# Gates of a bidirectional recurrence made where the projections end, with its diagonal, two copies and a scaling moved to other places

## The chip, the cores and the metric

The kernel runs on one core of a Trainium2 chip. A core has a matrix engine (TensorE, "PE" in the profile), a vector engine (VectorE, "DVE"), a scalar engine (ScalarE, "ACT"), GpSimd ("POOL"), and a synchronisation engine (SyncE, "SP") that here only issues transfers. Transfers are also issued from GpSimd, where they can add to what lies at the destination. Each engine works through its own queue in order; semaphores tie the queues together. The metric is the device time of one execution in microseconds, with the median over several runs.

## What is computed

One layer of an encoder trunk on 1024 positions of 1024 values in float32. After an RMS norm, one projection makes the columns of all token mixers. A convolution branch (GLU, 31 taps, LayerNorm, swish, pointwise product) and a bidirectional gated linear recurrence (HGRN2, 8 heads of 128) run on them, are gated, merged and projected; a gated feed-forward block with a 3-tap convolution follows. The parts that the change touches:

```python
def _forget_log_and_key(z, lb):
    zf = z.astype(jnp.float32)
    f = lb + (1.0 - lb) * jax.nn.sigmoid(zf)
    lf = jnp.log(jnp.clip(f, MIN_FORGET, 1.0))
    key_gate = (1.0 - lb) * jax.nn.sigmoid(-zf)
    return lf, key_gate

def _token_mixers(...):
    proj = jnp.einsum("bsd,de->bse", h, w_in)
    glu_in, q, v, z_f, z_b, og, g_a, g_b = jnp.split(proj, SPLIT_POINTS, axis=-1)
    a = jax.nn.glu(glu_in, axis=-1)
    a = _dwconv_centred(a, dw_w, dw_b)
    a = jax.nn.silu(_layernorm(a, ln_w, ln_b))
    a = jnp.einsum("bsc,cd->bsd", a, pw_w)
    o = _bi_hgrn2(q, v, z_f, z_b, lb[0], lb[1])
    of = o * lax.rsqrt(jnp.mean(o * o, axis=-1, keepdims=True) + EPS)
    of = of.reshape(o.shape[0], o.shape[1], HGRN_WIDTH) * norm_w.astype(jnp.float32)
    bmix = (of * jax.nn.silu(og.astype(jnp.float32))).astype(h.dtype)
    ...
```

For each head and direction the recurrence is `S_t = diag(f_t) S_{t-1} + k_t v_t^T`, `o_t = S_t^T q_t`. The kernel evaluates it for halves of 512 positions: inside blocks of 8 positions by two products, and across blocks by levels of 8, 16, 32 and 64.

## The kernel before

A product of float32 matrices is made of three passes: each operand is split into a high part (a cast on ACT, L121) and the remainder (a subtraction, mostly on DVE, L118), and L143 to L145 multiply high by high, high by low, low by high.

The stages follow one another with overlaps.

- *Projections in pairs* (up to about 480 us). `pair_job` (L224 to L285) makes two columns of 128 outputs for both halves with seven products instead of eight. Sums of weight blocks are made by accumulating transfers issued from GpSimd (L238). Products are gathered in three PSUM banks; `copy` (L266) takes partial sums p1, u2 and p7 out with ACT, and `evac` hands each quadrant (column, half) to the column's own function, in the order (0,0), (1,1), (1,0), (0,1). Of the seventeen pairs, 0 to 7 make q and the output gates, 8 to 16 make v, zf and zb of heads 0 to 5 (the list `todo`). `store` (L584) is the function of all these columns: DVE combines two partial sums (L588) into one of the three `ev` pages, or ACT copies a bank (L593), and SP writes the page to memory.
- *Convolution branch* beside it: the 31 taps on DVE (L645), then, for each half, the LayerNorm (L662 to L701): a mean (L672), a subtraction on DVE (L674), four squares on ACT into the four `tm` pages (L678), their sum on POOL (L657, L659), column sums on PE (L420), the rstd on POOL (L404, L405), its spread to all partitions (L411 to L413), and scale, shift and swish (L685 to L687). `s_pairs.fill(n)` puts n steps of the pair jobs between these.
- *Scan* (about 545 to 1000 us): 8 heads of two halves. `scan_inputs` loads q and z, makes k and f on ACT, and clamps f on DVE; `scan_base` makes cumulative products inside the blocks of 8, in the tile `DE`; `scan_levels` makes the 128 x 128 score blocks S, one level at a time, with masks; `scan_states` and `outputs` make the states that are carried; `scan_outputs` makes the head's outputs, their norm and gate. `between` (L1022) interleaves, after each step, dense projection steps (heads 6 and 7, merge gates), two steps of the next half's base, and one of the previous head's outputs.
- *Output projections, feed-forward up* (to about 1610 us), not touched.
- *Down projection*: five groups (4, 4, 5, 5, 4 blocks of 128 rows); `load_g` (L1234) loads and splits the next group's activations while the present one is multiplied.

The order of PE's instructions is written out by hand: it is the order in which the program calls them. The order on the other engines is a scheduler's. Pages of a pool are reused when their readers are done: `tm` has four, `ev` three.

Of the kernel before, what the change touches and what calls it, by code (L numbers as in the profile page):

```python
# [44 lines left out]
def tile_hybrid_encoder(  # L45
# [60 lines left out]
    def ev():  # L106
        return page(mp, "ev", 3)
# [280 lines left out]
    d_z = scratch("d_z", 2, NH, 2)  # L388
# [168 lines left out]
    m_32 = cp.tile([P, P], U8, name="m_32")  # L557

    def build_masks():
# [16 lines left out]
        for m, h in ((m_16, 16.0), (m_32, 32.0)):  # L576
            V.tensor_scalar(fs[:, 2, :], fs[:, 0, :], h, None, op0=ALU.is_ge)
            V.tensor_scalar(fs[:, 3, :], fs[:, 0, :], 2 * h, None, op0=ALU.is_lt)
            V.tensor_tensor(m, fs[:, 2, :], fs[:, 3, :], op=ALU.mult)
# [4 lines left out]
    def store(dst, func=None):  # L584
# [12 lines left out]

    todo = [
# [10 lines left out]
        for t in (  # L609
            (OFF_V + h * DK, store(d_v[h])),  # L610
            (OFF_ZF + h * DK, store(d_z[0][h])),
            (OFF_ZB + h * DK, store(d_z[1][h])),
# [128 lines left out]
    def scan_inputs(i):  # L741


# [3 lines left out]
        kk = hp.tile([P, 2, H], F32, tag="k", name=nm("k"), bufs=2)  # L747
        nc.sync.dma_start(q, d_q[h][half])
        for d in range(2):
            z = page(hp, "zi", 3)  # L750
            nc.sync.dma_start(z, d_z[d][h][half])
            A.activation(kk[:, d, :], z, AF.Sigmoid, scale=-1.0)
            A.activation(z, z, AF.Sigmoid)
            fo = view(f, d * H + 7 * d, [[8, NB], [1 - 2 * d, 8]])
            A.activation(
                fo,
                z.rearrange("p (b e) -> p b e", e=8),
                AF.Identity,
                scale=oml_of(d, h),
                bias=lb_of(d, h),  # L760
            )
        V.tensor_scalar(f, f, MIN_FORGET, 1.0, op0=ALU.max, op1=ALU.min)
        return q, f, kk, kscale[:, h : h + NH + 1 : NH]

    def scan_base(ins):
# [14 lines left out]
        V.tensor_copy(ed(2, D + 4), fv(3, 4))  # L780
# [44 lines left out]
    def scan_levels(base, S_t, Tt):  # L825
# [31 lines left out]
        for h in (8, 16, 32, 64):  # L857
# [10 lines left out]
            elif h < 64:  # L868
                V.copy_predicated(S_t, over(m_16 if h == 16 else m_32), b)
# [15 lines left out]
        V.tensor_tensor(S_t, S_t, c4(dg), op=ALU.add)  # L885
# [40 lines left out]
    def scan_outputs(h, kept, Sf, Sb):  # L926


        ons, gates = [], [load(d_og[h][half]) for half in range(2)]
        for half in range(2):  # L930
# [22 lines left out]
            for c in range(4):  # L953
                sl = slice(c * P, (c + 1) * P)
                A.activation(on[:, sl], on[:, sl], AF.Copy, scale=rs[:, c : c + 1])
            ons.append(on)
            yield
        for half in range(2):
            if half:
                yield  # L960
# [365 lines left out]
    for n, group in enumerate(groups):  # L1326
        last = n == len(groups) - 1
        for hs in ((0,), (1,)) if last else ((0, 1),):
# [4 lines left out]
            if not last:  # L1333
                load_g(f0 + group, groups[n + 1])
# [36 lines left out]
```

## Time and profile before

| | us |
|---|---|
| median of three runs | 1889.1 (1888.84 to 1890.98) |
| the profiled execution's own time | 1889.98 |
| its span in the trace | 1888.2 |
| TensorE busy | 1790.4 |
| VectorE busy | 1270.7 |
| ScalarE busy | 797.8 |
| GpSimd busy | 212.4 |
| mean granted TensorE clock | 0.982 |

How to read it: the page gives for each engine its busy time, its share of the span and its instructions. A group line gives line, engine, operation, tiles and shape, then the busy time and the mean of one in ns, and behind the second bar the idle time of the engine ahead of these instructions with what ended it. A line of waits says which engine waited at which line for which other, in total, how often, and the longest. A line of the timeline has the start in the span, the duration, and in brackets the idle time before. "PEld" is the loading of weights, which overlaps the products. "d_z", "d_q" and the like are scratch arrays in memory.

### The profile page before, as it was taken

Reading aid. Unit: us, or ns where it says so; the run is one execution under the profiler, and the core shown is the slowest. Engines: PE = TensorE matmul, PEld = TensorE weight load, DVE = VectorE, ACT = ScalarE, POOL = GpSimd, SP = SyncE. Lnnn points to the kernel's source line nnn. Section 1 sums busy time; section 2 is a strip of 40 time slices with the busy share of each in tenths; the row PEclk is TensorE's granted clock in tenths of the full one; section 3 lists DMA queues with packets and bytes.
Section 4 is the critical chain, followed back from the end, with each engine's and each line's share of the span. In section 5 each row is a group of like instructions: output and inputs, shape, how many; then the busy total and the mean of one; then the engine's idle time right before and its main releaser. Section 6 shows DMA issues by size and latency. Waiting matters only on the chain. (4 is left out here: it accounts for less than half of the span.)

```text
span 1888.2 us, 23731 instructions
## 1 busy us (share of the span) xinstructions
PE 1790.4 (95%) x8543; PEld 1477.7 (78%) x8543; DVE 1270.7 (67%) x1860; ACT 797.8 (42%) x1488; POOL 212.4 (11%) x218
## 2 busy tenths in 40 slices
PE   6988999999999999999999999899999999899996
PEld 5767888877788887888877888678888888788885
DVE  3488999535469898999936555766676666534445
ACT  6333343234555555665443134544343434522124
POOL 3101111213100001000000000211111111000000
PEclk8999999999999999999999999999999999999998
DMA  7747788776562333332228665777676665733125
GB/s 261 221 118 169 182 195 195 180 180 159 185 200 85 117 97 106 112 110 81 82 69 251 193 197 174 178 159 154 145 156 147 146 148 129 218 96 95 55 85 167
DMA packets 322764, 282.99 MB, mean 150 GB/s; under 512 B 14798, under 2 KB 244950, under 8 KB 322646
## 3 DMA queue, kind: packets, MB, share of 16 engines
q1 hardware_dynamic: 270854, 240.57, 41.1%
q0 software_dynamic: 51792, 40.90, 15.3%
q8 instruction: 67, 1.10, 0.2%
q14 instruction: 51, 0.42, 0.1%
HBM read 189.14 MB, written 71.83 MB: 138 GB/s over the span
## 5 line engine op out<-in xcount | busy, mean ns | idle before, releaser
L143 PE MATMUL mm<-hx,wp 128*128 128x512 f32 x1176 | 481.1, 409 | 21.9 <-ACT xr L1244 4.8
L145 PE MATMUL mm<-hx,wp 128*128 128x512 f32 x1176 | 466.6, 397 | 4.6 <-DVE wp L118 4.6
L144 PE MATMUL mm<-hx,wp 128*128 128x512 f32 x1176 | 466.5, 397 | 2.1 <-POOL hx L118 1.9
L121 ACT CAST wp<-wr 128x1024 fp32r<-128x1024 f32 (+2 forms) x196 | 179.6, 917 | 337.9 <-PE mm L144 203.7
L118 DVE TENSOR_TENSOR wp<-wr,wp 128x1024 fp32r<-128x1024 f32 (+2 forms) x196 | 207.0, 1056 | 119.9 <-ACT wp L121 114.3
L143 PEld LDWEIGHTS mm<-hx,wp 128*128 128x128 f32 x1176 | 225.7, 192 | 72.2 <-ACT su L266 5.8
L145 PEld LDWEIGHTS mm<-hx,wp 128*128 128x128 f32 x1176 | 225.1, 191 | 55.7 <-DVE wp L118 6.7
L144 PEld LDWEIGHTS mm<-hx,wp 128*128 128x128 f32 x1176 | 225.7, 192 | 47.7 <-POOL hx L118 3.6
L645 DVE SCALAR_TENSOR_TENSOR acc<-gl,v_b,acc 128x1024 f32<-128x1024 f32 x120 | 149.1, 1277 | 0.5
L238 POOL DMA_DIRECT2D wr<-sw x39 | 34.9, 895 | 512.9 <-DVE wp L118 251.9
L1250 DVE TENSOR_TENSOR xr<-mm,xr 128x512 f32<-128x512 f32 x48 | 33.2, 691 | 82.0 <-PE mm L145 81.9
L838 PEld LDWEIGHTS sc<-qF,A 128*128 128x128 f32 x512 | 65.3, 192 | 19.1 <-issue 13.3
L838 PE MATMUL sc<-qF,A 128*128 128x128 f32 x512 | 68.2, 276 | 11.7 <-DVE qF L730 10.6
L121 ACT CAST wq<-sw 128x1024 fp32r<-128x1024 f32 x39 | 41.0, 1051 | 80.0 <-PE mm L144 62.8
L143 PE MATMUL mm<-hy,wp 128*128 128x512 f32 x156 | 62.2, 399 | 8.9 <-ACT wp L121 5.9
L835 ACT COPY A<-kG 128x512 f32<-128x512 f32 x64 | 39.7, 621 | 66.6 <-DVE kG L730 38.0
L1172 DVE SCALAR_TENSOR_TENSOR tm<-gp,v_a,tm 128x512 f32<-128x512 f32 x88 | 65.6, 746 | 1.7 <-ACT tm L1168 0.9
L266 ACT COPY su<-mm 128x512 f32<-128x512 f32 x78 | 45.4, 581 | 48.7 <-PE mm L145 48.5
L144 PE MATMUL mm<-hy,wp 128*128 128x512 f32 x156 | 61.8, 396 | 0.0
L145 PE MATMUL mm<-hy,wp 128*128 128x512 f32 x156 | 61.3, 393 | 0.0
L143 PE MATMUL tr<-hx,wp 128*128 128x512 f32 x156 | 61.2, 392 | 0.0
L143 PE MATMUL sc<-hy,wq 128*128 128x512 f32 x156 | 61.1, 392 | 0.0
(289 smaller groups left out, 3602.1 us busy)
## 6 DMA issues: line engine op xcount, KB each, us to landing
wr<-in_w_in_dram SPq DMA_DIRECT2D x55, 512.0 KB, 6.6
sw<-in_ffn_w_up_dram SPq DMA_DIRECT2D x44, 256.0 KB, 4.1
sw<-in_ffn_w_up_dram POOLq DMA_DIRECT2D x22, 512.0 KB, 8.5
wr<-in_ffn_w_up_dram SPq DMA_DIRECT2D x22, 512.0 KB, 4.9
d_g<-ft SPq DMA_DIRECT2D x44, 256.0 KB, 5.9
ev<-d_g SPq DMA_DIRECT2D x44, 256.0 KB, 3.1
wr<-sw POOLq DMA_DIRECT2D x39, 256.0 KB, 3.3
wr<-wr POOLq DMA_DIRECT2D x39, 256.0 KB, 4.4
```

Of the source, the lines that this page charges most:

```text
L118: eng.tensor_tensor(lo, src, hi.bitcast(F32), op=ALU.subtract)
L121: A.copy(hi, src)
L143: T.matmul(acc, whi[:, k, :], ahi, start=first, stop=False, skip_group_check=again)
L144: T.matmul(acc, whi[:, k, :], alo, start=False, stop=False, skip_group_check=again)
L145: T.matmul(acc, wlo[:, k, :], ahi, start=False, stop=last, skip_group_check=again)
L238: G.dma_start(o, a, accum_op=ALU.add)
L266: A.copy(t, acc)
L645: V.scalar_tensor_tensor(acc, g[:, k : k + S], tap(k), acc, op0=ALU.mult, op1=ALU.add)
L835: A.copy(A_t.rearrange("p (b x e) -> p b x e", x=2, e=h), pairs(kG, h))
L838: T.matmul(b[:, c * P : (c + 1) * P].rearrange("p (b x e) -> p b x e", x=2, e=h), A_t[:, c * P : (c + 1) * P], view(qF, c * P, [[2 * h, P ...
L1172: V.scalar_tensor_tensor(c, g[:, o + k : o + k + H], vec("fdw", k * NF + j), c, op0=ALU.mult, op1=ALU.add,)
L1250: V.tensor_tensor(xr[i][half], acc, xr[i][half], op=ALU.add)
```

## The change

- The z columns get a function of their own, `gates`, in place of `store`: ACT makes k = sigmoid(-z), sigmoid(z) and f = lb + (1 - lb) sigmoid(z) (for the backward direction with the positions of each block of 8 reversed), DVE clamps f, and SP stores k and f in the new scratch arrays `d_k` and `d_f`. k and f take `tm` pages, sigmoid(z) an `ev` page. `scan_inputs` only loads.
- In `scan_base` the two columns that start the products are copied by ACT instead of DVE.
- In `scan_levels` the level of 32 is no longer put in under a mask by DVE, but copied by ACT in four pieces of 32 partitions, as the level of 64 is in two; the mask goes.
- The diagonal `dg` is added to S by an accumulating transfer from GpSimd instead of by DVE.
- In `scan_outputs` the output gates get pages of their own, and a half's scaling by its rstd is called later: half 0's after the squares of half 1, half 1's a step after that. The output transposes of both halves follow with one step between the halves' ends less than before.
- In the down projection the next group's loads are put between the matmul steps, nine steps after the first three and then one block every four.

```diff
-    d_z = scratch("d_z", 2, NH, 2)
+    d_k = scratch("d_k", 2, NH, 2)
+    d_f = scratch("d_f", 2, NH, 2)
...
+    def gates(d, h):
+        def evac(half, x0, x1=None, op=None):
+            if x1 is not None:
+                t = ev()
+                V.tensor_tensor(t, x0, x1, op=op)
+                x0 = t
+            k, sg, f = tmp(), ev(), tmp()
+            A.activation(k, x0, AF.Sigmoid, scale=-1.0)
+            A.activation(sg, x0, AF.Sigmoid)
+            nc.sync.dma_start(d_k[d][h][half], k)
+            A.activation(
+                view(f, 7 * d, [[8, H // 8], [1 - 2 * d, 8]]),
+                sg.rearrange("p (b e) -> p b e", e=8),
+                AF.Identity,
+                scale=oml_of(d, h),
+                bias=lb_of(d, h),
+            )
+            V.tensor_scalar(f, f, MIN_FORGET, 1.0, op0=ALU.max, op1=ALU.min)
+            nc.sync.dma_start(d_f[d][h][half], f)
+        return evac
...
-            (OFF_ZF + h * DK, store(d_z[0][h])),
-            (OFF_ZB + h * DK, store(d_z[1][h])),
+            (OFF_ZF + h * DK, gates(0, h)),
+            (OFF_ZB + h * DK, gates(1, h)),
...
+        for d in range(2):
+            nc.sync.dma_start(f[:, d, :], d_f[d][h][half])
         nc.sync.dma_start(q, d_q[h][half])
         for d in range(2):
-            z = page(hp, "zi", 3)
-            nc.sync.dma_start(z, d_z[d][h][half])
-            A.activation(kk[:, d, :], z, AF.Sigmoid, scale=-1.0)
-            A.activation(z, z, AF.Sigmoid)
-            fo = view(f, d * H + 7 * d, [[8, NB], [1 - 2 * d, 8]])
-            A.activation(
-                fo,
-                z.rearrange("p (b e) -> p b e", e=8),
-                AF.Identity,
-                scale=oml_of(d, h),
-                bias=lb_of(d, h),
-            )
-        V.tensor_scalar(f, f, MIN_FORGET, 1.0, op0=ALU.max, op1=ALU.min)
+            nc.sync.dma_start(kk[:, d, :], d_k[d][h][half])
...
-        V.tensor_copy(ed(2, D + 4), fv(3, 4))
+        A.copy(ed(2, D + 4), fv(3, 4))
...
-            elif h < 64:
-                V.copy_predicated(S_t, over(m_16 if h == 16 else m_32), b)
+            elif h == 16:
+                V.copy_predicated(S_t, over(m_16), b)
             else:
                 for s0 in range(0, P, h):
                     t0 = s0 ^ h
...
-        V.tensor_tensor(S_t, S_t, c4(dg), op=ALU.add)
+        G.dma_start(S_t.rearrange("p c t -> p (c t)"), dg, accum_op=ALU.add)
...
-        ons, gates = [], [load(d_og[h][half]) for half in range(2)]
+        ons, outs = [], []
+        for half in range(2):
+            outs.append(page(hp, "og", 2))
+            nc.sync.dma_start(outs[half], d_og[h][half])
+
+        def scale(on, rs):
+            for c in range(4):
+                sl = slice(c * P, (c + 1) * P)
+                A.activation(on[:, sl], on[:, sl], AF.Copy, scale=rs[:, c : c + 1])
...
-            for c in range(4):
-                sl = slice(c * P, (c + 1) * P)
-                A.activation(on[:, sl], on[:, sl], AF.Copy, scale=rs[:, c : c + 1])
-            ons.append(on)
-            yield
+            if half == 0:
+                ons.append((on, rs))
+                yield
+            else:
+                scale(*ons[0])
+                ons.append((on, rs))
+        yield
+        scale(*ons[1])
         for half in range(2):
-            if half:
-                yield
             b = bank("tr")
...
             if not last:
-                load_g(f0 + group, groups[n + 1])
+                st.fill(9)
+                for f in range(f0 + group, f0 + group + groups[n + 1]):
+                    load_g(f, 1)
+                    st.fill(4)
             st.drain()
```

More of the change, by code (lines that the diff above doesn't have):

```diff
@@ L556, in tile_hybrid_encoder @@
     m_16 = cp.tile([P, P], U8, name="m_16")
-    m_32 = cp.tile([P, P], U8, name="m_32")
     def build_masks():
@@ L575, in build_masks @@
         V.tensor_tensor(m_b, fs[:, 2, :], fs[:, 3, :], op=ALU.mult)
[L576 to L579, printed above, removed]
+        V.tensor_scalar(fs[:, 2, :], fs[:, 0, :], 16.0, None, op0=ALU.is_ge)
+        V.tensor_scalar(fs[:, 3, :], fs[:, 0, :], 32.0, None, op0=ALU.is_lt)
+        V.tensor_tensor(m_16, fs[:, 2, :], fs[:, 3, :], op=ALU.mult)
     build_masks()
```

4 lines of the change are left out of this document (2 added, 2 removed).

## The prediction

> **What bounds the kernel now.** I read the page first, then the windows by stage, then the waits of the scan, and last the timeline around the LayerNorm of the conv branch. The page says who has no spare time:
>
> ```profile
> span 1888.2 us, 23731 instructions
> PE 1790.4 (95%) x8543; PEld 1477.7 (78%) x8543; DVE 1270.7 (67%) x1860; ACT 797.8 (42%) x1488; POOL 212.4 (11%) x218
> ```
>
> TensorE is idle for 1888.2 - 1790.4 = 97.8 us. No edit takes a matmul away, so all that can be won lies in these idle stretches and in the clock that is lost after them. The windows say where they lie and who is full there:
>
> ```profile
> 560.00:940.00 380.00, 356.27 (x2256) 312.58 (x2254) 352.41 (x652) 202.27 (x459) 25.64 (x26) 0.99 0.32 98
> 940.00:960.00 20.00, 17.36 (x99) 14.57 (x99) 9.56 (x19) 10.15 (x29) 1.20 (x2) 0.91 0.38 118
> 160.00:340.00 180.00, 177.68 (x778) 145.64 (x779) 175.84 (x166) 69.39 (x98) 31.80 (x28) 1.00 0.82 188
> 1620.00:1640.00 20.00, 15.21 (x58) 12.02 (x57) 12.62 (x20) 10.73 (x21) 0.00 (x0) 0.83 0.83 260
> ```
>
> The columns after the length are PE, PE weight loads, DVE, ACT, POOL, the granted clock, the DMA share and GB/s. In the scan (560 to 940, on to 960) DVE is busy for 352.4 of 380 us, and PE is idle for 380 - 356.27 + 20 - 17.36 = 26.4 us. The clock of 0.99 over 380 us and 0.91 over 20 loses another 3.8 + 1.8 = 5.6 us. From 160 to 340 (projections beside conv taps) DVE is even fuller, yet PE idles only 2.3 us: its weights are ready ahead. The stretch at 1620 is the start of the down projection: 4.8 us idle and a clock of 0.83. The waits from 440 to 960, each as total, times and longest:
>
> ```profile
> ACT A L835 <- DVE kG L730: 38.0, 22, 4.6
> ACT tm L955 <- POOL ors L405: 24.0, 14, 4.0
> DVE kG L730 <- ACT A L835: 12.9, 7, 3.7
> PE sc L838 <- DVE qF L730: 9.8, 8, 2.8
> PE tr L894 <- ACT kT L896: 7.4, 3, 2.9
> PE tr L894 <- DVE ev L965: 4.0, 3, 1.8
> ```
>
> PE waits for DVE directly 9.8 + 4.0 us. The 7.4 us for kT are ACT's, and ACT itself is late because it waits for DVE's kG (38.0 us): three of the four ends lead to DVE.
>
> **What the change takes out of the scan.** The rows that carry it:
>
> ```profile
> L752 ACT ACTIVATE k<-zi 128x512 f32<-128x512 f32 x32 | 19.0, 623 | 18.4 <-DVE Kh L733 13.7 <-DMA zi<-d_z 4.6
> L753 ACT ACTIVATE zi<-zi 128x512 f32<-128x512 f32 x32 | 19.6, 624 | 0.1
> L755 ACT ACTIVATE f<-zi,lbw 128x512 f32<-128x512 f32 x32 | 25.9, 815 | 0.1
> L762 DVE TENSOR_SCALAR f<-f 128x1024 f32<-128x1024 f32 x16 | 11.0, 686 | 13.7 <-ACT f L755 13.7
> L869 DVE COPY_PREDICATED S<-m,sc 128x512 f32<-128x512 uint8 x32 | 23.3, 727 | 0.7 <-PE sc L838 0.7
> L885 DVE TENSOR_TENSOR S<-S,dg 128x512 f32<-128x512 f32 x16 | 10.9, 680 | 1.8 <-ACT S L873 1.8
> L780 DVE COPY DE<-f 128x256 f32<-128x256 f32 x16 | 6.8, 427 | 0.0
> L923 ACT COPY Sb<-sc 128x128 f32<-128x128 f32 x8 | 2.2, 274 | 0.0
> L238 POOL DMA_DIRECT2D wr<-wr x39 | 33.4, 856 | 115.8 <-DMA wr<-sw 113.8 <-DMA cx<-d_cv 1.9
> L686 DVE TENSOR_SCALAR cx<-cx,v_a 128x512 f32<-128x512 f32 x8 | 4.1, 541 | 0.0
> ```
>
> DVE loses per half of a head the clamp (0.686), one of two predicated copies (0.727), the diagonal (0.680) and the column copy (0.427): 2.52 us, 40.3 over 16 halves. The clamp comes back in half size, 32 times; I take 0.41 us, between half of L762's 0.686 and the 0.541 of L686. Eight of the 32 stand in the scan's dense jobs (heads 6 and 7), 3.3 us. Net -37 us of DVE, 2.3 per half. ACT loses 19.0 + 19.6 + 25.9 = 64.5 us and gets 8 gates of 0.623 + 0.624 + 0.815 = 2.06 us (16.5), 64 level-32 copies at the 0.274 of L923 (17.5) and 16 column copies near DVE's 0.427 (6.8): net -23.7. POOL gets 16 accumulating DMAs; by L238 one holds it for 0.86 us, 14 us in all on an engine with 25.6 of 380 busy. S is read only when its head's outputs are made, a head later, so the landing is hidden; uncovered it would cost a landing per head. That issue can stand ahead of the rstd that L955 waits for, 0.86 us each; with 16 at worst on the path, 14 us is the far end.
>
> The sixteen halves lie between about 548 and 940, 24.5 us each, so 560 to 940 holds 15.5. DVE's busy time becomes 352.4 - 15.5 x 2.3 = 316.7; with its 12.9 us of waiting for A, 329.6, against PE's 356.3. PE would set the pace, with 26.7 us to spare, 1.7 per half. Bounds of the gain: 26.4 + 5.6 = 32 at most, and nothing at all if new waits fill the room. I take the two waits on DVE and the one behind kT, 9.8 + 4.0 + 7.4 = 21.2, and the same share of the clock, 5.6 x 21.2/26.4 = 4.5: **-25.7**. The postponed scaling I put at nothing: in the built order it stands where it stood, behind the squares of its half, for half 0 in most heads, and ACT goes on waiting for POOL; PE's order changes by the second half's output transposes alone, one step earlier.
>
> **What it puts into the projections.** 24 of the 32 gates fall into pairs 8 to 16, which end at about 482 with the evacuation of 482.46 below. In the conv part each adds 0.41 us to a full DVE; the ends are 0 and 12 x 0.41 = 4.9, and I take 0 because PE waited only 2.3 us in 180. The writes double from 24 to 48 of 256 KB there; ends 0 and a few tenths each, taken as nothing. The two LayerNorm halves are another matter: the ACT order now has gates ahead of the squares (L678), and PE's order, written by hand, has the column sums (L420) at a fixed place. First half, before:
>
> ```profile
> 432.57 0.69 DVE L588 TENSOR_TENSOR ev<-su,mm 128x512 f32<-128x512 f32 x1 [0.34 <-ACT tm L678]
> 436.45 0.68 DVE L588 TENSOR_TENSOR ev<-sc,su 128x512 f32<-128x512 f32 x1
> 437.77 1.04 ACT L121 CAST wp<-wr 128x1024 fp32r<-128x1024 f32 x1 [1.87 <-PE mm L144]
> 438.73 0.58 ACT L593 COPY ev<-mm 128x512 f32<-128x512 f32 x1
> 433.82 1.61 POOL L657 TENSOR_TENSOR tm<-tm,tm 128x512 f32<-128x512 f32 x1
> 435.51 3.84 POOL L659 TENSOR_TENSOR tm<-tm,tm 128x512 f32<-128x512 f32 x2
> 440.97 1.59 POOL L238 DMA_DIRECT2D sw<-in_w_in_dram  x1 [1.62 <-DVE r L424]
>   PE ob L420: 1.5, 1
> ```
>
> POOL's sum ended at 435.51 + 3.84 = 439.35 and PE had waited 1.5 us: it was there at 437.9. After: the quadrant that DVE hands over at 437.13 gets its gate on ACT till 439.2, the cast of 1.04 till 440.2, then one square, the v copy (0.58) and a second square: 442.0; POOL's 1.61 + 3.84 end at 447.5. PE waits 9.6 instead of 1.5, +8.1. The transfer of 1.59 us that stood on POOL ahead of the rstd has then gone out before; I give back 1.4. **+6.7**. The squares also need the four tm pages that k and f of both quadrants hold. The last f is stored about 439.6, and its page is free when it has landed:
>
> ```profile
> d_z<-ev SPq DMA_DIRECT2D x32, 256.0 KB, 2.0
> ```
>
> that is 441.6, just before the last square; if SP holds the store behind the weight load, each microsecond counts in full. This is the far side of the term.
>
> Next comes the copy of u2 (L266). PE needs it for product 5:
>
> ```profile
> 452.78 0.54 DVE L686 TENSOR_SCALAR cx<-cx,v_a 128x512 f32<-128x512 f32 x1
> 453.82 0.39 PE L143 MATMUL mm<-hy,wq 128*128 128x512 f32 x1
> L752 ACT ACT_TABLE_LOAD x1 | 1.3, 1283 | 0.0
> ```
>
> On ACT there now stand before it both pairs of silus and casts, a load of the table, and two sigmoids of a gate: from 453.3 (the last L686) 1.15 + 1.13 + 1.28 + 1.25 + 0.58 = 458.7, against 453.82. **+4.9**. It is nothing only if the DVE part comes 5 us earlier. The price of such a load is 1283 ns in the row. The Trainium skill (ScalarE: Activation LUTs, What ACT_TABLE_LOAD costs) adds about 1380 ns of drain to the 1283 and so speaks against mixing sigmoid and silu. This row doesn't show the drain; by the page the stall would be 6.3 and the forecast 1.4 later.
>
> Second half:
>
> ```profile
> 479.40 0.69 DVE L588 TENSOR_TENSOR ev<-sc,su 128x512 f32<-128x512 f32 x1 [1.04 <-PE sc L145]
> 482.46 0.58 ACT L593 COPY ev<-mm 128x512 f32<-128x512 f32 x1
> 476.00 2.49 ACT L678 ACTIVATE tm<-cx 128x512 f32<-128x512 f32 x4 [2.35 <-DVE cx L674]
> 478.68 2.66 POOL L659 TENSOR_TENSOR tm<-tm,tm 128x512 f32<-128x512 f32 x2
> 483.29 0.95 PE L420 MATMUL ob<-ones_m,tm 128*128 128x1 f32 x8
> ```
>
> The squares, at 476.0 before, now stand behind three gates. The last reads its bank directly, from about 482.5: 1.25, a cast of 0.62, 0.815, then the squares to 487.7; POOL's sum, two adds of 2.66 after the last square, ends at 490.4, against 483.29. **+7.1**. After an idle stretch of 4.8 us the clock of the 1620 row is 0.83: 32 of 90 matmuls are missing there, 7.1 us, 2.3 more than the idle. I charge that to the two LayerNorm stalls, **+4.6** (ends 0 and three times 2.3).
>
> **The down phase.** PE's idle there is the wait in the page's first group:
>
> ```profile
> L143 PE MATMUL mm<-hx,wp 128*128 128x512 f32 x1176 | 481.1, 409 | 21.9 <-ACT xr L1244 4.8
> ```
>
> The next group's loads are spread between the matmul steps. But in the built order only one of 34 casts has moved from before the first xr copies to behind them. Ends 0 and the whole 4.8 + 2.3 = 7.1; I take **-3**.
>
> **Sum.** 6.7 + 4.9 + 7.1 + 4.6 - 25.7 - 3 = -5.4. From the profiled execution's 1889.98 that is 1884.6; the median of the runs, 1889.1, lies 0.9 below it: **1883.7**.
>
> **Rivals.** *All of the scan's idle goes.* PE is then the bound from 560 to 960, the down stall is gone too, and the clock stays up at the three new stalls: 1889.1 + 18.7 - 32 - 7.1 = 1868.7. For it speaks DVE's 1.7 us of room per half; against it, 24.0 us of ACT waiting for POOL that nothing removes. Chance 0.17.
>
> *ACT's column copy stops DVE: slower.* The copy into DE was DVE's own; now DVE hands f to ACT and has to wait two operations later. In several heads it stands on ACT behind the scale that waits for POOL, or behind level-32 copies. Queued behind it on DVE are the reciprocal and all of the next half's base. DVE has 1.7 us of room per half; above that each us costs 16. The wait is between the copy alone (0.43) and the longest POOL wait plus it (4.4); at 3.0 it takes (3.0 - 1.7) x 16 = 20.8, and the time is 1904.5. Against it: ACT is only 202 of 380 us busy. Chance 0.24.
>
> *The gain is smaller than the waits say:* kT(0) now stands on ACT behind the second scale, so its 7.4 us stay, with 1.6 of clock, and the spread loads do nothing, as one moved cast suggests: 1883.7 + 9.0 + 3.0 = 1895.7. Chance 0.12.
>
> *The scaling and the loads don't do what they say and the LayerNorm takes back the rest:* within the 0.2% (3.8 us) that a measurement can tell from no change. Chance 0.13.
>
> **How the numbers follow.** The forecast itself has 0.34, own range 1874 to 1885. Faster: 0.34 + 0.17 = 0.51; same 0.13; slower 0.24 + 0.12 = 0.36. The low end, 1867, is the first rival with a little of the LayerNorm's price off; the high end, 1905, is the column copy at 3 us. Outside lie about 0.05 below and 0.13 above.
>
> **What will show it.** Windows 420 to 500: PE idle of 10, 5 and 7 us at L420 (now waiting for POOL) and at the copy of u2, four more table loads, a clock below 1. Scan: DVE below 330 us in a window of the same work, qF and ev waits of PE nearly gone, L955 still waiting for POOL, DE <- ACT among DVE's waits at under 1.7 us. Down: the wait for xr at 3 us less. I am wrong if L420 doesn't wait, since then the gain is 20 us larger, or if PE's waits for qF stay.

## The result, and the profile after

| | us |
|---|---|
| kernel before, median on the same chip | 1888.97 (1884.23 to 1890.98, 4 runs) |
| changed kernel, median | 1940.34 (1935.38 to 1941.82, 4 runs) |
| ratio | 1.0271, 95% interval 1.0244 to 1.0298 |
| profiled execution of the changed kernel | 1939.18, span 1937.4 |

The change makes the kernel slower by 2.7%, some 51 us. The forecast was 1883.7, with a range that ended at 1905. The page of the changed kernel:

```profile
span 1937.4 us, 24013 instructions
PE 1810.9 (93%) x8543; PEld 1492.4 (77%) x8543; DVE 1250.0 (65%) x1825; ACT 827.5 (43%) x1558; POOL 234.8 (12%) x234
```

TensorE has the same 8543 matmuls, but stands idle for 126.5 us instead of 97.8, and its busy time has grown by 20.5 us: the same work at a colder clock, 0.971 granted on the mean instead of 0.982. To see where, take the marks of the program from the view of single lines: the first LayerNorm mean (L695, before L672), the first level product of the scan (L850, before L838) and the last output transpose (L985, before L963). Behind the three durations stand the first and the last start:

```profile
L695 PE MATMUL ob<-tm,ones_m x4: 591/592/592, 436.0 to 498.0; 128*128 128x512 f32 x4
L850 PE MATMUL sc<-qF,A x512: 270/275/348, 593.8 to 1018.1; 128*128 128x128 f32 x171
L985 PE MATMUL tr<-ident,tm x64: 270/328/477, 655.4 to 1049.7; 128*128 128x128 f32 x64
```

With the same marks of before, and the first accumulation of the down projection (1672.5 before, 1721.2 after), the span falls into five pieces:

| piece | before | after | difference | forecast |
|---|---|---|---|---|
| start to the first LayerNorm mean | 428.7 | 436.0 | +7.3 | 0 |
| to the first level product | 130.2 | 157.8 | +27.6 | +23.3 |
| scan, to the last output transpose | 439.3 | 455.9 | +16.6 | -25.7 |
| to the first down accumulation | 674.3 | 671.5 | -2.8 | |
| the rest of the down projection | 215.7 | 216.2 | +0.5 | -3 (with the piece above) |
| sum | 1888.2 | 1937.4 | +49.2 | -5.4 |

The piece of the LayerNorm lost 27.6 us where 23.3 were forecast, and the piece ahead of it 7.3 where nothing was. The large error is the scan: 42 us between +16.6 and -25.7. Five of the rows of TensorE's waits in the changed kernel (total, times, longest) name the places:

```profile
PE tr L985 <- ACT tm L949: 23.2, 7, 4.4
PE ob L421 <- POOL tm L682: 16.1, 2, 10.0
PE mm L143 <- ACT su L266: 13.8, 7, 4.0
PE sc L850 <- DVE qF L753: 6.1, 7, 1.1
PE mm L143 <- ACT xr L1266: 3.3, 1, 3.3
```

The first line is new: output transposes (L985) that wait for the scaling (L949); the row of before, L963 for L955, had 1.9 us. The second is the LayerNorm's column sum, forecast. The fourth was 9.8 us in the scan: TensorE waits less for VectorE than before. The windows over the scan, before and after (columns as in the prediction), say the same:

```profile
558.90:998.20 439.30, 410.14 (x2563) 358.42 (x2562) 376.07 (x694) 230.11 (x533) 30.88 (x33) 0.98 0.32 99
```

```profile
593.80:1049.70 455.90, 419.00 (x2562) 364.12 (x2561) 349.67 (x638) 218.41 (x544) 51.89 (x48) 0.97 0.42 125
```

VectorE lost 26 us of work here (376.07 to 349.67; 37 were forecast), ScalarE 12, and the scan became longer. So in the changed kernel VectorE's work does not set the length of the scan; whether it did before, the experiments have to say.

One head shows the new wait. The timeline of the changed kernel between 713 and 722 us, on TensorE, ScalarE and GpSimd (start, duration, line, and in brackets the wait):

```profile
718.24 1.36 PE L985 MATMUL tr<-ident,tm 128*128 128x128 f32 x4 [3.67 <-ACT tm L949]
719.73 1.11 PE L906 MATMUL tr<-ident,kG 128*128 128x128 f32 x4
720.50 0.78 PE L143 MATMUL mm<-hx,wp 128*128 128x512 f32 x1
721.07 0.63 PE L144 MATMUL mm<-hx,wp 128*128 128x512 f32 x1
```

```profile
715.52 0.60 ACT L847 COPY A<-kG 128x512 f32<-128x512 f32 x1
717.78 1.28 ACT L949 ACTIVATE tm<-tm,ors 128x128 f32<-128x128 f32 x4 [1.66 <-POOL ors L406]
```

```profile
715.05 0.91 POOL L897 DMA_DIRECT2D S<-dg  x1 [3.99 <-ACT S L885]
716.04 0.19 POOL L405 TENSOR_SCALAR ors<-oss 128x4 f32<-128x4 f32 x1
716.31 1.44 POOL L406 TENSOR_TENSOR ors<-ors,mhalf 128x4 f32<-128x4 f32 x1
```

Half 1's rstd is ready at 717.75, ScalarE has waited 1.66 us for it, and TensorE, whose order now has these transposes one step earlier, stops for 3.67 us. The matmul at 721.07 takes 0.63 us where one took 0.39 at 714: the granted clock is 0.50 from 718.24 to 722 and 0.63 to 726, after 0.99 before. So this wait cost more than its length.

In the LayerNorm the forecast's chain can be read off line by line. ScalarE, then GpSimd, then TensorE of the changed kernel, first half:

```profile
444.50 0.81 ACT L609 ACTIVATE tm<-ev,lbw 128x512 f32<-128x512 f32 x1
448.51 1.04 ACT L121 CAST wp<-wr 128x1024 fp32r<-128x1024 f32 x1 [3.20 <-DMA wr<-wr]
449.46 0.62 ACT L701 ACTIVATE tm<-cx 128x512 f32<-128x512 f32 x1
452.46 0.63 ACT L701 ACTIVATE tm<-cx 128x512 f32<-128x512 f32 x1 [0.85 <-POOL tm L680]
472.42 1.28 ACT L606 ACT_TABLE_LOAD   x1
474.77 0.57 ACT L266 COPY su<-mm 128x512 f32<-128x512 f32 x1
```

```profile
452.51 2.60 POOL L682 TENSOR_TENSOR tm<-tm,tm 128x512 f32<-128x512 f32 x2
```

```profile
455.17 1.86 PE L421 MATMUL ob<-ones_m,tm 128*128 128x1 f32 x8 [9.95 <-POOL tm L682]
475.39 0.50 PE L143 MATMUL mm<-hy,wq 128*128 128x512 f32 x1 [3.96 <-ACT su L266]
```

The squares (L701) stand behind the gates and a cast, the column sum waits 9.95 us, and the copy of u2 at 474.77 stands behind a table load and holds TensorE for 3.96. Not all of the 9.95 us is the gates': they end at 445.31, when TensorE has just begun to wait, and the cast behind them then waits 3.20 us for its weights. In the kernel with the late transposes below, that wait is 2.04 and the column sum's 8.79: the same 1.16 us less. The last of the four squares also waited for a page that POOL's first sum had to give back (0.85), so the four pages count a little too. Behind the load that began at 472.42 the next instruction starts 1.30 us later, so nothing shows here of the drain that the prediction mentioned beside the load.

### The profile page after: what moved, and what is told of

It is laid out like the page before. It is cut to its first block, busy times and chain, and to the rows that moved or that the text cites. A ratio compares the mean times of both kernels' runs of the same rounds, so it can differ in the third digit from the quotient of the medians.

```text
span 1937.4 us, 24013 instructions
## 1 busy us (share of the span) xinstructions
PE 1810.9 (93%) x8543; PEld 1492.4 (77%) x8543; DVE 1250.0 (65%) x1825; ACT 827.5 (43%) x1558; POOL 234.8 (12%) x234
## 5 line engine op out<-in xcount | busy, mean ns | idle before, releaser
L121 ACT CAST wp<-wr 128x1024 fp32r<-128x1024 f32 (+2 forms) x196 | 179.6, 917 | 313.2 <-PE mm L144 210.3
L121 ACT CAST wq<-sw 128x1024 fp32r<-128x1024 f32 x39 | 41.0, 1051 | 84.7 <-PE mm L144 69.4
L850 PEld LDWEIGHTS sc<-qF,A 128*128 128x128 f32 x512 | 65.3, 191 | 12.8 <-issue 8.9
L850 PE MATMUL sc<-qF,A 128*128 128x128 f32 x512 | 68.1, 276 | 6.2 <-DVE qF L753 6.1
L1178 DVE TENSOR_TENSOR ft<-su,mm 128x512 f32<-128x512 f32 x22 | 15.1, 688 | 73.6 <-issue 70.1
```

The lines of the kernel that those rows point to most:

```text
L121: A.copy(hi, src)
L850: T.matmul(b[:, c * P : (c + 1) * P].rearrange("p (b x e) -> p b x e", x=2, e=h), A_t[:, c * P : (c + 1) * P], view(qF, c * P, [[2 * h, P ...
```

## The experiments

All times of a row are against runs of the kernel before on the same chip, so ratios are compared; "scan" is the piece of the table above, from the profiled execution of each kernel.

**Undoing single parts of the change.** Half 1's transposes put back to their old step, the scaling left late:

```diff
         scale(*ons[1])
         for half in range(2):
+            if half:
+                yield
             b = bank("tr")
```

> The changed kernel with one step put back between the output transposes of the two halves, so that half 1's transposes stand on PE where they stood before; the scaling stays a step later. Theory A (PE's order is the cause: half 1's transposes, one step earlier, wait for a scale that waits for POOL's rstd): most of PE's 23.2 us of waiting at L985 goes, and the colder clock after these waits; 1940 becomes about 1910 (1900 to 1918), with L985 waiting under 6 us. Theory B (the moved scaling itself is late, wherever the transposes stand): half 0's transposes still wait and the time stays above 1930. Theory C (ACT's column copy holds up DVE): 1935 to 1942, no change.

Measured: ratio 1.0151 (1.0128 to 1.0175) against 1.0271, 1.2% or some 22 us back, and the scan 439.1 us instead of 455.9. L987 (the transposes) waits only 0.6 us for the scale. Theory A holds, B and C fall: ScalarE's column copy made DVE wait 9.0 us in all, before and after this edit alike. But 439.1 is just what the scan took before the change. Where did VectorE's 26 us go? The waits of this kernel in the scan:

```profile
ACT tm L949 <- POOL ors L406: 28.4, 14, 4.4
PE tr L906 <- DVE ev L989: 16.8, 7, 3.6
PE sc L850 <- DVE qF L753: 5.0, 6, 1.1
```

The next wait is L906's, for the bank that DVE's `ev` has to empty, 16.8 us; before the change this pair of lines had 4.0.

Scaling and transposes both as before:

```diff
-            if half == 0:
-                ons.append((on, rs))
-                yield
-            else:
-                scale(*ons[0])
-                ons.append((on, rs))
-        yield
-        scale(*ons[1])
+            scale(on, rs)
+            ons.append((on, rs))
+            yield
         for half in range(2):
+            if half:
+                yield
```

> The changed kernel with scaling and transposes both at the steps of the kernel before (each half scaled right behind its rstd; only the own pages for the output gates stay). Theory A: the same as with the late transposes alone, within 4 us. Theory B: clearly faster than that, 1905 or less where the late transposes alone stay above 1930. Theory C: no change.

Measured: 1.0173 (1.0146 to 1.0200), scan 438.3. The intervals of this and of the late transposes overlap, and the medians are 4.9 us apart where theory A allowed 4: it is TensorE's order; where the program calls the scaling makes no difference that is shown.

The diagonal added by DVE again:

```diff
-        G.dma_start(S_t.rearrange("p c t -> p (c t)"), dg, accum_op=ALU.add)
+        V.tensor_tensor(S_t, S_t, c4(dg), op=ALU.add)
```

> The changed kernel with the diagonal added by DVE again. Theory D (the transfer's issue, 0.91 us on POOL, stands ahead of half 1's rstd, so that the scale and the transposes are late by it): 7 heads by 0.5 to 0.9 us, 4 to 7 us faster. Theory A: 0 to 3 us faster, since the issue delays the rstd only 0.4 us in the head looked at, and DVE has room for the 11 us.

Measured: 1.0247 (1.0225 to 1.0270), scan 452.8, 3.1 shorter. The intervals of this and of the changed kernel overlap, and two executions with the same code in the scan differ by as much (below); if the transfer costs anything, it is the few us of theory D and not the main thing.

z stored and the gates made in the scan (the diff of the change, with `gates`, `d_k`, `d_f` and `scan_inputs` as before):

> The changed kernel with z stored and the gates made in the scan again, as before; all other parts of the change stay. If the LayerNorm's waits come from the gates ahead of the squares, the mean of the second half starts about 23 us earlier than in the changed kernel and L421 waits 2 us or less, and the projections end 33 us earlier. The scan gets 64 us of ACT and 11 of DVE back: by theory A it still waits at the transposes, and loses 5 to 15 us more there. Sum 1912 to 1925.

Measured: 1.0174 (1.0152 to 1.0196). The first mean is at 425.5, the first level product at 555.1 instead of 593.8, and L420 waits 1.8 us: the loss in the projections is the gates', all of it. The scan takes 469.1, 13 more than with the gates moved, inside the range.

**What holds the scan at 439?** Level 32 back on DVE, on top of the late transposes:

```diff
...
-            elif h == 16:
-                V.copy_predicated(S_t, over(m_16), b)
+            elif h < 64:
+                V.copy_predicated(S_t, over(m_16 if h == 16 else m_32), b)
```

> The changed kernel with the late transposes and with level 32 put in by DVE under its mask again. In the late-transposes kernel the scan (first level product to last output transpose) took 439.1 us, as before the change, with L906 waiting 16.8 us for DVE's ev. Theory E (ACT's four level-32 copies stand between the four squares of the outputs and make the rstd, the scale, the next A and so ev late): the scan gets 6 to 15 us shorter, L906's wait for ev falls under 8 us, the ratio to before falls from 1.015 to about 1.008 to 1.012. Theory F (the chain over POOL's rstd itself holds the scan, wherever the copies are made): scan within 3 us of 439.

Measured: 1.0165 (1.0142 to 1.0189), scan 439.1, L908 (the kG transposes) still waiting 15.9 us for `ev`. Theory E falls.

Level 32, the two columns and the diagonal all on DVE:

```diff
-        A.copy(ed(2, D + 4), fv(3, 4))
+        V.tensor_copy(ed(2, D + 4), fv(3, 4))
...
```

> The changed kernel with the late transposes and with level 32, the two columns and the diagonal all made by DVE again: of the scan's edits only the gates stay moved. Theory E: at least as short as with level 32 alone, scan 420 to 432. Theory F: 439 again. Rival G (DVE is the bound, as my prediction had it, and gets 29 us back): scan 445 or more, and PE waiting over 10 us for qF.

Measured: 1.0136 (1.0120 to 1.0151), scan 434.1, between the numbers of E and F; G, which asked for 445 or more, falls. In the scan VectorE is busy for 19 us more than with the late transposes (367.6 against 348.3), yet the scan is not longer. The wait has changed its name again, from `ev` to kT, and stayed:

```profile
ACT tm L951 <- POOL ors L406: 33.7, 14, 5.7
PE tr L908 <- ACT kT L910: 9.9, 3, 4.9
PE tr L908 <- DVE ev L991: 6.1, 3, 3.2
```

What is in all these kernels is the line above: ScalarE waits some 30 us in the scan for GpSimd's rstd, with A, kT and, through A, DVE's kG and `ev` queued behind it.

**The LayerNorm.** The squares and their sum called ahead of the six pair steps, with the late transposes:

```diff
-        s_pairs.fill(LN_FILL)
         sqs = [tmp() for _ in xs]
         for sq, t in zip(sqs, xs):
             A.activation(sq, t, AF.Square)
-        rstd = rstd_over_partitions(total(sqs, sqs[0]), CW, "ob", tmp())
+        sq_sum = total(sqs, sqs[0])
+        s_pairs.fill(LN_FILL)
+        rstd = rstd_over_partitions(sq_sum, CW, "ob", tmp())
```

> The changed kernel with the late transposes, and with the LayerNorm's squares and their sum called ahead of the six pair steps instead of behind them, so that on ACT they stand ahead of the gates. If the gates ahead of the squares are the LayerNorm's loss, L421's 15 us of waiting goes to under 4 us and the projections end 12 to 20 us earlier; the copy of u2 still waits about 4 us. If it is the four tm pages, the gates now wait for the squares' pages, ACT stops there, and less than 6 us come back.

Measured: 1.0041 (1.0018 to 1.0065), first level product at 566.9 instead of 586.2. TensorE's waits in the projections are now

```profile
PE mm L143 <- ACT su L266: 8.4, 7, 4.0
PE ob L421 <- POOL tm L682: 2.2, 1, 2.2
```

so the order of squares and gates on ScalarE was nearly all of the loss at L421, and the four pages were not.

The same with the copies and the diagonal on DVE:

> The squares ahead and the copies and diagonal on DVE together: gates moved, late scaling, spread loads of the down phase. If both theories hold the gains add: ratio to before 0.992 to 1.002. If the tm pages hold the LayerNorm, 1.005 or more.

Measured: 1.0072 (1.0046 to 1.0097), scan 436.3. The gains do not add: theory E had no gain to give.

**The wait for the rstd.** Transposes still later, on the squares-ahead kernel:

```diff
-            if half == 0:
-                ons.append((on, rs))
-                yield
-            else:
-                scale(*ons[0])
-                ons.append((on, rs))
-        yield
-        scale(*ons[1])
+            ons.append((on, rs))
+            yield
         for half in range(2):
-            if half:
-                yield
+            scale(*ons[half])
+            yield
             b = bank("tr")
```

> The squares-ahead kernel with the output transposes of half 0 one step and of half 1 two steps later still, so that PE reaches them, and the bank that they share with the kG transposes, later. Theory F (PE waits for the chain squares, POOL's rstd, scale on ACT, then A and ev behind it): the transposes themselves wait for nothing, and the waits of L907 for ev shrink, since ev no longer sits between two kG transposes; scan 425 to 434 instead of 438.8. If the wait only moves on to A and kT, 436 to 442.

Measured: 1.0105 (1.0085 to 1.0124), slower than the squares-ahead kernel, of which the scan (441.4) shows only a part. It is the case "the wait only moves on":

```profile
PE tr L907 <- ACT kT L909: 20.8, 7, 5.5
```

kT stands on ScalarE behind the scaling. Now the rstd and the scaling left out:

```diff
-            rstd_small(rs, ss, DK)
...
-            for c in range(4):
-                sl = slice(c * P, (c + 1) * P)
-                A.activation(on[:, sl], on[:, sl], AF.Copy, scale=rs[:, c : c + 1])
+            return
```

> The squares-ahead kernel without the rstd and the scaling of the outputs (left out: POOL's two operations and ACT's four scalings per half; the outputs go on unscaled). Theory F: ACT's 28 us of waiting for POOL and 20 us of scaling are gone, A, kT and ev come 2 to 3 us earlier in each half, and PE's waits in the scan fall from about 29 us to under 12: scan 418 to 426. If the scan stays above 434, neither the rstd nor the scaling holds it, and theory F falls.

Measured: ratio 0.9908 (0.9884 to 0.9932), scan 411.8: 27 us. And the scaling done, but by a constant:

```diff
-                A.activation(on[:, sl], on[:, sl], AF.Copy, scale=rs[:, c : c + 1])
+                A.activation(on[:, sl], on[:, sl], AF.Copy, scale=ones_m[:, c : c + 1])
```

> The squares-ahead kernel with each scaling done, but by a column of ones in place of the rstd (POOL still makes the rstd, and nobody waits for it; what is left out is the norm's factor). Without rstd and scaling the scan was 411.8 us against 438.8. If the wait for POOL holds the scan, nearly all comes back here too: 410 to 420. If it is ACT's own 20 us of scaling, the scan stays at 430 or more. Half and half: 420 to 430.

Measured: 0.9899 (0.9872 to 0.9927), scan 412.4. The 20 us of scaling cost nothing that can be seen; the wait for GpSimd costs it. (With the dependence gone the scheduler also ordered ScalarE's queue anew. In one head A, the scaling and kT stood at 738.92, 741.46 and 742.76, and now the scaling comes first, at 731.42, with kT at 733.00 and A at 734.91. The wait and the order that it forces are not told apart.) The windows of the scan, with the late transposes (whose code there is that of the squares-ahead kernel) and with the constant:

```profile
586.20:1025.30 439.10, 410.45 (x2562) 359.60 (x2561) 348.25 (x636) 216.31 (x542) 51.26 (x48) 0.98 0.44 130
567.60:980.00 412.40, 399.83 (x2563) 353.30 (x2562) 349.26 (x637) 215.60 (x542) 52.94 (x48) 1.00 0.46 139
```

VectorE has as much to do (349.3 and 348.3), TensorE is idle for 12.6 us instead of 28.7, and the clock is 1.00 instead of 0.98.

And the same constant in the kernel before the change, whose scaling is otherwise untouched:

> The kernel before the change, with each scaling of the outputs done by a column of ones in place of POOL's rstd (left out: the norm's factor). In the changed kernel with the squares ahead this made the scan 412.4 us instead of 438.8. If DVE's relief is worth nothing anywhere, the scan here falls by the same 26 us, to 410 to 416. If POOL's wait and DVE's load hold the scan one behind the other, DVE becomes the bound here and the scan stays at 424 or more; the difference to 412.4 is then what the moved gates and copies are worth once the wait is gone.

Measured: 0.9954 (0.9937 to 0.9972), scan 426.4, the second case. TensorE's two large waits there are for VectorE:

```profile
PE sc L838 <- DVE qF L730: 9.1, 9, 2.8
PE tr L894 <- DVE ev L965: 8.6, 6, 2.2
```

So the wait for GpSimd costs the scan 13 us with the edits of the old kernel and 26 with those of the new. Without the wait the scan is 426.4 us before and 412.4 after: all of the change's edits in the scan together, with ScalarE's relief from the gates, are then worth 14 us. What VectorE's share of that is, no run tells.

**The table loads.** Swish as x times sigmoid(x), on the squares-ahead kernel:

```diff
-            A.activation(xn, xn, AF.Silu)
+            sg = ev()
+            A.activation(sg, xn, AF.Sigmoid)
+            V.tensor_tensor(xn, xn, sg, op=ALU.mult)
```

> The squares-ahead kernel with the LayerNorm's swish made as x times sigmoid(x) (a product of 128x512 on DVE, eight in all) so that no activation table is loaded between the gates. If the two loads of 1.28 us and the gate behind them are what makes u2 late, the wait of 4.0 us at the copy of u2 falls under 1.5 and the projections end 3 to 6 us earlier, ratio 0.999 to 1.002. If the gates alone make it late, no change.

Measured: 1.0027 (1.0013 to 1.0040) against 1.0041 (1.0018 to 1.0065): the intervals overlap, so no gain in the time is shown. The scan took 435.9 us, with the code in it that took 438.8. In the trace the first level product comes 4.3 us earlier (562.6) and the longest wait for an su copy falls from 4.0 to 2.4 us, less than expected.

All of the change but the gates and the earlier transposes:

> The changed kernel with z stored and the gates made in the scan, and with the late transposes: all of the change but the gates and the earlier transposes. The projections end as before the change. With ACT 64 us fuller again, theory F gives a scan of 436 to 445 and a ratio of 0.995 to 1.005; if the gates were worth what my prediction gave them, 450 or more.

Measured: 1.0078 (1.0062 to 1.0095), scan 453.0. The projections are as before (first level product at 557.4), and the scan is 13.7 longer than before: with the gates back in it, the rest of the change makes it worse. That is the second case, in which the gates are worth what the prediction gave them. Against the late-transposes kernel the moved gates save 13.9 in the scan (453.0 to 439.1) and cost 28.8 in the projections (557.4 to 586.2).

Side by side, the scans of the kernels in which the transposes stand where they stood:

| scan, us | copies and diagonal on VectorE | copies on ScalarE, diagonal by GpSimd's transfer |
|---|---|---|
| gates in the scan | 439.3 (before) | 453.0 |
| gates in the projections | 434.1, 436.3 | 439.1, 438.8, 435.9 |

Kernels in one cell have the same code in the scan, so differences of 3 us are not told from chance. The equality of 439.3 and 439.1 is thus no fixed floor, but two steps that cancel: the gates taken out save time behind the wait too, and the copies put on ScalarE, with the diagonal's transfer, cost time. They cost most where ScalarE was fullest: in the kernel of 453.0 it is busy for 253.5 us, and VectorE waits 30.7 us for the gates' f, where it waited 4.8 before the change.

**A version that is faster than both.** One rstd for both halves of a head, after half 1's squares, both scalings behind it (on the squares-ahead kernel with swish from sigmoid; `ss` and `rs` have eight columns for a head):

```diff
-            rstd_small(rs, ss, DK)
...
+        rstd_small(rs, ss, DK)
+        scale(*ons[0])
         yield
         scale(*ons[1])
```

> The kernel with squares ahead and swish from sigmoid, and one rstd for both halves of a head, made after half 1's squares; both halves are scaled after it, and half 0's transposes come a step later. In the built order two A copies now stand ahead of the scalings. ACT waits for POOL once in a head instead of twice. If the wait for POOL with A queued behind it is the cause, the scan falls from 436 to 420 to 428 and the ratio to before is 0.988 to 0.998. If the time goes to the banks that the output transposes share with kG's, as with the transposes two steps later, 436 to 442 and a ratio of 1.002 to 1.008.

Measured: 1.0064 (1.0040 to 1.0088), scan 432.2: the ratio of the second case, the scan between both. The A copies now pass ahead of the wait, and the waits for GpSimd are halved. But TensorE meets the scaled halves too early again, and the piece from the last output transpose to the first down accumulation is 7.3 us longer than with the swish from sigmoid (678.4 against 671.1), where TensorE now waits 9.7 us for a cast (hx, L121):

```profile
PE tr L987 <- ACT tm L954: 13.6, 7, 2.7
ACT tm L954 <- POOL ors L406: 15.3, 8, 2.6
```

With half 1's transposes in the step after half 0's:

```diff
         for half in range(2):
-            if half:
-                yield
             b = bank("tr")
```

> As the joint rstd, with half 1's transposes a step earlier, in the step after half 0's. If the transposes wait for the scale again, 5 us or more above the joint rstd; if only the banks' order matters, within 5 us of it either way.

Measured: 1.0072 (1.0052 to 1.0092), scan 435.5, L985 waiting 14.1 us: no difference to the joint rstd that is shown.

The transposes two steps behind the scalings, and the last head without the added steps:

```diff
         scale(*ons[0])
-        yield
         scale(*ons[1])
+        if h < NH - 1:
+            yield
+            yield
         for half in range(2):
-            if half:
-                yield
             b = bank("tr")
```

> Squares ahead, swish from sigmoid, one rstd per head, both halves scaled after it, and half 0's transposes a step later than with the joint rstd (where they waited 13.6 us for the scale); half 1's in the next step; the last head's tail not lengthened. If the wait for POOL is the cause to the end, the 13.6 us and the 7 us of the tail go: scan 416 to 425, ratio 0.988 to 0.997, faster than both kernels. If the wait moves on once more, scan 430 or more and a ratio of 1.000 or more.

Measured: 0.9984 (0.9965 to 1.0003), scan 427.3: between the two cases, the transposes' wait mostly gone and 2 to 11 us of the hoped-for scan missing.

With a step between the halves' transposes, except in the last head:

```diff
         for half in range(2):
+            if half and h < NH - 1:
+                yield
             b = bank("tr")
```

> As the one with later transposes, with a step between the two halves' transposes. The order of the shared banks against kG's transposes is the only difference: within 5 us of the other; whichever has kG's transposes next to an output's waits more at L909.

Measured: 0.9973 (0.9958 to 0.9989), median 1879.95 against 1885.16 of the kernel before on the same chip; scan 425.1. It gains 14.2 us in the scan, and the projections hand over 10.2 later than before (first level product at 569.1). This is the one complete version that is shown faster than both kernels; the one before it beats by 0.3%. In its scan no wait of TensorE is large:

```profile
PE sc L853 <- DVE qF L756: 6.4, 7, 1.8
PE sc L918 <- ACT kT L911: 3.9, 4, 1.8
PE tr L989 <- ACT kT L911: 3.6, 2, 1.9
PE tr L989 <- ACT tm L954: 3.1, 3, 2.1
```

## Why the prediction was wrong, point by point

*What bounds the scan: wrong, and the error that mattered.* The prediction read three of four waits back to VectorE (qF, ev, and kT through A behind kG) and took all 21.2 us of them as gained. The line that held the scan was quoted beside them, ScalarE's 24.0 us of waiting for GpSimd's rstd, and was only used as an argument against a rival. TensorE waits for kT and ev as soon as ScalarE or VectorE is late, and both queue behind that wait. So with the gates moved and the transposes at their old step or later, the waits changed names from kernel to kernel (ev, kT) while the scan stayed at 434 to 441, and 19 us of VectorE's work more or less did not show. Where the prediction had -25.7, the kernel with the late transposes has -0.2 (439.3 to 439.1). Taking out the wait gave 26 us in the changed kernel with squares ahead and late transposes, and 13 in the old one. A wait on an engine that is 11% busy was counted as something that "nothing removes", and not as what held the scan. The prediction also overlooked that ScalarE, whose queue stands behind that wait, is not free to take more: where it still makes the gates, the copies put on it, with the diagonal's transfer, made the scan 13.7 us longer (439.3 to 453.0).

*VectorE's relief: mis-sized.* In the scan its busy time fell by 26.4 us and not by 37. The working took the durations of rows from a busy time, but VectorE's instructions overlap: one of those shown further below begins at 873.97 and takes 1.22 us, and the next begins 1.14 us after it. The rows listed for the scan's window add up to 427 us before and 394 after, for busy times of 376.1 and 349.7. The result doesn't hang on it, since no run shows time that the relief of VectorE alone bought.

*The scaling "at nothing": wrong.* The working said that TensorE's order changes by half 1's transposes alone, one step earlier, and gave this no price. The step back is worth 16.8 us of scan, as the late transposes show (455.9 to 439.1). With a hand-written order, an instruction moved ahead must be checked against what it waits for. Half 1's scale stood behind the same rstd, too late for its old place by little (1.9 us in two waits), and for the new one by up to 4.4 us.

*The LayerNorm: right in its mechanism, and in one size by luck.* Column sums +6.7 and +7.1: waits of 10.0 and 6.1, where 1.5 and none stood. The first agrees because two errors cancel: the cast's 3.20 us of waiting for its weights was not in the working, and GpSimd's part behind the last square took 2.0 us (453.09 to 455.11) instead of the 5.45 that it had. The u2 copy +4.9: 3.96. The colder clock was mis-sized, with +4.6 forecast. From the first mean to the first level product TensorE waits 21.8 us (16.1 + 4.0 + 1.7) instead of 2.2, and the piece grew by 27.6, so 8.0 are left that no wait carries. They are about the clock's: for the same 548 matmuls TensorE is busy for 136.1 us instead of 127.9, with 0.90 granted instead of 0.99. The squares called ahead of the gates took 14.9 us of waiting down to 2.2.

*The conv part "at nothing": probably wrong by some us.* In the executions with the gates in the projections the first mean lies between 428 and 438, in those without between 425.5 and 429.6; the two ranges overlap a little. In the changed kernel's execution it came 7.3 later. TensorE's waits for su copies there went from 2.9 to 7.1 us, p1, u2 and p7 now standing behind gates on ScalarE, but all its waits there only from 14.6 to 17.5, so most of the 7.3 has no cause shown. The prediction had looked for the price on VectorE, at the clamps.

*The down phase: not to be told.* Forecast -3; the wait for xr went from 4.8 to 3.3 us, and the two last pieces of the table together are 2.3 shorter, less than they differ between executions of the later kernels, which share this code.

*The rivals.* The slower rival was the column copy stopping VectorE: it cost VectorE 9.0 us of waiting in three places, up to 3.1 us in one, and the time nothing that the runs show. Its 1904.5 was the nearest number, 36 us short of the time, and for a cause that no run shows; that it lies nearest is luck. The rival of a wholly free scan came near only with the norm's factor left out, where 12.6 us of idle stayed. Of the prediction's two signs of being wrong, L420 (now L421) did wait, and the waits for qF stayed in part: 6.1 us of 9.8.

## What to carry to other kernels

Before a wait is credited to the engine it names, follow it through the queues: here two engines late behind one small operation on a third showed as many different waits, and taking work from VectorE only renamed the wait, while the work that was given to ScalarE, in whose queue the wait stood, cost time where that queue was fullest. A cheap test is to cut the suspected dependency with a constant, in both kernels; here it separated 26 us of waiting from 20 us of work that cost nothing visible. And where one engine's order is fixed by hand, an instruction put ahead of what it needs can cost more than the other engines gain: here its waits and the clock after them took 16.8 us.

## What the hardware showed that was not expected

GpSimd's first operation of the rstd works on 4 columns and took 0.19 us at best, but up to 3.49, in the view of single lines of the changed kernel (shortest, median, longest in ns), with one such case, the scaling that waited for it, and what VectorE did in most of that time:

```profile
L405 POOL TENSOR_SCALAR ors<-oss x16: 187/368/3486, 649.7 to 1039.3; 128x4 f32<-128x4 f32 x16
```

```profile
873.69 3.48 POOL L405 TENSOR_SCALAR ors<-oss 128x4 f32<-128x4 f32 x1 [20.11 <-ACT jk L969]
```

```profile
878.31 1.28 ACT L949 ACTIVATE tm<-tm,ors 128x128 f32<-128x128 f32 x4 [3.83 <-POOL ors L406]
```

```profile
873.97 1.22 DVE L753 TENSOR_TENSOR qF<-Qh,fm 128x1024 f32<-128x1024 f32 x1
875.11 1.22 DVE L753 TENSOR_TENSOR kG<-Kh,DE 128x1024 f32<-128x1024 f32 x1
876.24 0.25 DVE L753 TENSOR_TENSOR tb<-tb 128x96 f32<-128x96 f32 x1
876.41 0.71 DVE L753 TENSOR_TENSOR DE<-f 128x256 f32<-128x256 f32 x1
```

It ended at 877.17, 0.05 us after VectorE's run of products of two SBUF operands. The three longest of the sixteen (3.49, 3.48 and 2.80 us) each ended 0.05 or 0.06 us after that same last product of the run (`DE<-f`). The Trainium skill (GPSIMD Engine Reference, Key points) says that GpSimd shares its SBUF interfaces with VectorE and contends with instructions of two SBUF inputs; these rows agree, though no run here took VectorE's products away from beside it, and the one at 765.60 took 0.19 us while such a product ran till 765.69. ScalarE waited 3.83 us for that rstd, of which 3.3 are this stretch. The kernel before the change has such stretches too (2.87 us, and 4.00 in the second operation). If VectorE's products are the cause, the wait that held the scan was in part their doing, by when they run and not by how many they are; that is not shown.
